# State-branch input matrices of a two-layer encoder: built transposed from table rows in scratch memory

## The chip, the cores and the metric

One core of one Trainium2 chip runs the whole kernel. The metric is the device time of one execution in microseconds (us), shown as the median of several runs. Engines are named as in the profile: PE is TensorE (PEld its weight loads), DVE is VectorE, ACT is ScalarE, POOL is GpSimd, SP is SyncE. L457 is line 457 of the kernel before.

## The reference, cut to what matters

An encoder of two layers over 512 tokens of width 2048, all float32. Each layer normalises, projects to 10272 columns, runs two token mixers side by side, a gated delta rule and a diagonal state-space branch ("state branch"), projects both, gates and adds them, and projects once more. The change is in the state branch. Per direction `d` it computes

```python
ug = u.reshape(bsz, L, N_GROUPS_B, S5_GROUP_CH)          # 64 groups of 16 channels
lam_bar = exp(lam * dt)                                   # complex, 64 states a group
b_bar = ((lam_bar - 1.0) / lam)[..., None] * (b_re + 1j * b_im)
bu = einsum('gpc,blgc->blgp', b_bar[d], ug)
states = associative_scan(_ssm_combine, (lam_bar, bu), axis=1, reverse=...)
y += einsum('gcp,blgp->blgc', c[d], states).real
```

## The kernel before, in words

**Dense products.** Every projection is cut into tiles of 128 output channels by 512 tokens. For each slice of 128 inputs there are three matmuls (L122, L123, L124), since weights and activations are split into a high and a low part in a reduced float32 format. `_weights` (L91) loads 8 slices of weights (`w_raw`, SP's queue, two buffers), ACT rounds them (`w_hi`, L65) and DVE takes the rest (`w_lo`, L66), three buffers each. A product fills one of three `acc` buffers in PSUM.

**The state branch** (`_s5`, L339) is traced at a raised priority beside the dense products, and the framework's scheduler writes one fixed order of instructions for each engine from modelled durations; an engine runs its list in order. Only the start, the delta-rule scan with its filler products, and the finish have PE's order written out by hand. Tokens are taken in 64 chunks of 8, so that only 64 steps of the recurrence are left. The 64 groups go in two halves (`hf`) of 32. In a half:

- *Parameters* (L361 to L424): `lam_in` and `b_in` are loaded; about 80 small DVE operations (`_exp_poly`, `_sincos`, L372 to L391) give the decay `lam_bar` and the scaled input matrix `b_bar`; the loop at L412 makes the powers 0 to 8 of `lam_bar`. All tiles have (real or imaginary, state) on the 128 partitions and (direction, group) along them.
- *Input matrices* (L445 to L464): eight sets `q` of four groups. For each direction `gen` (L429) multiplies `b_bar` with eight powers into `e_m`, of which the partitions are states. A matmul needs (lag, channel) on the partitions, so PE transposes each group's 128 by 128 block with the identity (L457, `ps_et`), ACT copies the four blocks back (`e_t`, L459), and `_halves` (L271) multiplies them with the input chunk `u_ch` into `ps_e`; ACT copies that to the state tile `h_st` (L464).
- *Recurrence* (L477 to L484): 64 steps of five small DVE operations.
- *Outputs* (L485 to L538): `gen` again for the output matrices `c_l`, short convolution kernels through a scratch tensor `d_k`, and products `ps_y`.

A half has its own pools of SBUF, in the memory that the half before or the last layer's final tiles leave free. All loads and stores of this branch and of the delta rule go through POOL's queue (`c.q`), in one fixed order: among them the stores `d_u` and `d_qk` of freshly projected tiles and the loads of the delta-rule scan.

**After it** come query, key and value tiles with a short convolution on DVE (`_qkv`), `_delta_pre`, `_delta_inv`, 46 gate tiles, the delta-rule scan (`_delta_scan`, L713) with other dense products between its steps, and last (L1128 on) the products with `w_pa` and `w_out`, whose split activations `m_h` and `m_l` take 64 KB of each partition.

Of the kernel before, what the change touches and what calls it, by code (L numbers as in the profile page):

```python
# [15 lines left out]
F32 = mybir.dt.float32  # L16
# [3 lines left out]
ALU = mybir.AluOpType  # L20
# [316 lines left out]

@with_exitstack
def _s5(ctx, c, l):  # L339
# [3 lines left out]
    HG = NG // 2  # L343
    pss = ctx.enter_context(tc.tile_pool(name=f"pss{l}", bufs=3, space=PSUM, reuse_waits="tile"))
    LOH, HIH = slice(0, 64), slice(64, 128)
    for hf in range(2):
        with ExitStack() as es:
            sp = es.enter_context(tc.tile_pool(name=f"s5_{l}_{hf}", bufs=1, reuse_waits="tile"))
            PW = [128, 2, HG]
            H = sp.tile([128, 2, HG, 65], F32, name="h_st")  # L350
            lr = sp.tile(PW + [9], F32, name="lam_r")
            lq = sp.tile(PW + [9], F32, name="lam_q")
            bp = sp.tile([128, 2, HG + 1, 16], F32, name="b_bar")
            bb = bp[:, :, 0:HG, :]
# [4 lines left out]
            bs = wk.tile(PW + [16], F32, name="b_swap", bufs=1)
            with tc.tile_pool(name=f"s5p_{l}_{hf}", bufs=1, reuse_waits="tile") as pp:  # L360
                lam = pp.tile([128, 3, 2, HG], F32, name="lam_in")  # L361
                b_in = pp.tile([128, 2, 2, HG, 16], F32, name="b_in")
                with tc.issue_after(c.x_load.ins) if (l, hf) == (0, 0) else nullcontext():
                    q = nc.sync if (l, hf) == (0, 0) else c.q
                    q.dma_start(out=lam, in_=i["s5_lam"][l, hf])
                    q.dma_start(out=b_in, in_=i["s5_b"][l, hf])
                mk = lambda nm: pp.tile(PW, F32, name=nm)
                re, im, ld = lam[:, 0], lam[:, 1], lam[:, 2]
                dt, t0, t1, mag = mk("p_dt"), mk("p_t0"), mk("p_t1"), mk("p_mag")
                l1r, l1i, fr, fi = mk("p_lr"), mk("p_li"), mk("p_fr"), mk("p_fi")  # L370
                _exp_poly(nc, pp, dt, ld, "d")
                V.tensor_tensor(out=t0, in0=re, in1=dt, op=ALU.mult)  # L372
                _exp_poly(nc, pp, mag, t0, "m")
                V.tensor_tensor(out=t0, in0=im, in1=dt, op=ALU.mult)
                _sincos(nc, pp, l1i, l1r, t0, "a")
                V.tensor_tensor(out=l1r, in0=l1r, in1=mag, op=ALU.mult)
                V.tensor_tensor(out=l1i, in0=l1i, in1=mag, op=ALU.mult)

                V.tensor_tensor(out=t0, in0=re, in1=re, op=ALU.mult)
                V.tensor_tensor(out=t1, in0=im, in1=im, op=ALU.mult)  # L380
                V.tensor_tensor(out=t0, in0=t0, in1=t1, op=ALU.add)
                V.reciprocal(out=dt, in_=t0)
                V.tensor_scalar(out=mag, in0=l1r, scalar1=-1.0, scalar2=None, op0=ALU.add)
                V.tensor_tensor(out=t0, in0=mag, in1=re, op=ALU.mult)
                V.tensor_tensor(out=t1, in0=l1i, in1=im, op=ALU.mult)
                V.tensor_tensor(out=t0, in0=t0, in1=t1, op=ALU.add)
                V.tensor_tensor(out=fr, in0=t0, in1=dt, op=ALU.mult)
                V.tensor_tensor(out=t0, in0=l1i, in1=re, op=ALU.mult)
                V.tensor_tensor(out=t1, in0=mag, in1=im, op=ALU.mult)
                V.tensor_tensor(out=t0, in0=t0, in1=t1, op=ALU.subtract)  # L390
                V.tensor_tensor(out=fi, in0=t0, in1=dt, op=ALU.mult)  # L391

                S16 = PW + [16]
                W16 = [128, 2, HG, 16]
                bt = bs
                sg = mk("p_sg")
                V.tensor_scalar(out=sg[LOH], in0=fi[LOH], scalar1=-1.0, scalar2=None, op0=ALU.mult)
                V.tensor_copy(out=sg[HIH], in_=fi[HIH])
                bcf = lambda a: _bc(a.unsqueeze(3), W16)
                V.tensor_tensor(out=bb, in0=b_in[:, 0], in1=bcf(fr), op=ALU.mult)  # L400
                V.tensor_tensor(out=bt, in0=b_in[:, 1], in1=bcf(sg), op=ALU.mult)
                V.tensor_tensor(out=bb, in0=bb, in1=bt, op=ALU.add)
                V.tensor_copy(out=bs[LOH], in_=bb[HIH])
                V.tensor_copy(out=bs[HIH], in_=bb[LOH])

                li = pp.tile(PW + [9], F32, name="lam_i")
                V.memset(lr[:, :, :, 0:1], 1.0)
                V.memset(li[:, :, :, 0:1], 0.0)
                V.tensor_copy(out=lr[:, :, :, 1], in_=l1r)
                V.tensor_copy(out=li[:, :, :, 1], in_=l1i)  # L410
                for k in range(2, 9):
                    a, b = k // 2, k - k // 2  # L412
                    V.tensor_tensor(out=t0, in0=lr[:, :, :, a], in1=lr[:, :, :, b], op=ALU.mult)
                    V.tensor_tensor(out=t1, in0=li[:, :, :, a], in1=li[:, :, :, b], op=ALU.mult)
                    V.tensor_tensor(out=lr[:, :, :, k], in0=t0, in1=t1, op=ALU.subtract)
                    V.tensor_tensor(out=t0, in0=lr[:, :, :, a], in1=li[:, :, :, b], op=ALU.mult)
                    V.tensor_tensor(out=t1, in0=li[:, :, :, a], in1=lr[:, :, :, b], op=ALU.mult)
                    V.tensor_tensor(out=li[:, :, :, k], in0=t0, in1=t1, op=ALU.add)
                neg = lambda o, a: V.tensor_scalar(out=o, in0=a, scalar1=-1.0, scalar2=None, op0=ALU.mult)
                neg(lq[LOH], li[LOH])  # L420
                V.tensor_copy(out=lq[HIH], in_=li[HIH])
                V.tensor_copy(out=q8[LOH], in_=li[LOH, :, :, 8])
                neg(q8[HIH], li[HIH, :, :, 8])
                V.tensor_copy(out=l8, in_=lr[:, :, :, 8])  # L424
# [4 lines left out]
            def gen(out, a, p, b, q, gs, d, ks, kn):  # L429
# [14 lines left out]
            h0 = H[:, 0, 0, 0:1]  # L444
            for q in range(8):  # L445
                j, g0 = hf * 4 + q // 2, q * 4
                gs = slice(g0, g0 + 4)
                if q % 2 == 0:
                    u = load_u(j)
                pe = pss.tile([128, 2, 4, 64], F32, name="ps_e", tag="ps")  # L450
                for d in range(2):
                    E = wk.tile([128, 4, 8, 16], F32, name="e_m", tag="e_m")
                    ks = slice(7, None, -1) if d == 0 else slice(0, 8)
# [31 lines left out]
            def kernels(jl):  # L485
# [13 lines left out]
                for q in range(2):  # L499
                    gl = slice(q * 4, q * 4 + 4)  # L500
                    gs = slice(jl * 8 + q * 4, jl * 8 + q * 4 + 4)
                    for d in range(2):
                        cm = C[q, d] = wk.tile([128, 4, 9, 16], F32, name=f"c_l{q}{d}", tag="c_l", bufs=CLB)
                        ks = slice(0, 9) if d == 0 else slice(8, None, -1)
                        gen(cm, ci[:, 0, d, gl], lr, ci[:, 1, d, gl], lq, gs, d, ks, 9)
# [446 lines left out]
def hybrid_encoder_kernel(ctx: ExitStack, tc: tile.TileContext, i: dict, out: bass.AP, dbg=None):  # L952
# [14 lines left out]
    c.d_u = dt("d_u", [8, 8, 128, 64])  # L967
    c.d_k = dt("d_k", [8, 2, 4, 32, 240])
# [70 lines left out]
    for l in range(DEPTH):  # L1039
# [142 lines left out]
def _layout(inp):  # L1182
# [43 lines left out]
    lam = np.empty((L, 2, 2, 64, 3, 2, 32), np.float32)  # L1226
    for q, nm in enumerate(("lam_re", "lam_im", "log_dt")):
        a = f[nm] if nm != "log_dt" else np.broadcast_to(f[nm][..., None], f["lam_re"].shape)
        a = a.reshape(L, 2, 2, 32, 64).transpose(0, 2, 4, 1, 3)
        lam[:, :, :, :, q] = a[:, :, None]  # L1230
# [50 lines left out]
```

## Time and profile before

| | us |
|---|---|
| median of 3 runs | 3087.45 |
| lowest, highest | 3082.66, 3088.57 |
| the profiled execution's own time | 3085.16 |
| its span, first to last instruction | 3083.3 |
| mean granted clock of TensorE, as a share of full speed | 0.995 |

The profile is one execution. "Busy" is the time in which an engine had an instruction running, except that matmuls overlap and their ends are modelled: a row's mean for one matmul is longer than what one adds to a dense stream. An engine's idle time matters only if that engine sets the end.

### The profile page before, as it was taken

The numbers are of one execution on the slowest core, as the hardware profiler recorded it, in microseconds if no ns is written. First come the engines' busy times: TensorE is split into PE (matmuls) and PEld (weight loads), VectorE is DVE, ScalarE is ACT, GpSimd is POOL, SyncE is SP. The second block draws the span as 40 slices with busy tenths as digits, with TensorE's granted clock in tenths as the row PEclk, the third lists the DMA queues.
The fourth block names the chain that finished last, engine by engine and source line by source line (L and its number), as shares of the span: only waits on it lengthen the run. The fifth ranks groups of instructions, "written<-read, shape, count | busy, mean of one in ns | idle before, by whom it ended". The sixth has DMA issues, their size and how long they took to land. (4 is left out here: it accounts for less than half of the span.)

```text
span 3083.3 us, 45415 instructions
## 1 busy us (share of the span) xinstructions
PE 3014.7 (98%) x17398; PEld 2387.5 (77%) x17398; DVE 2288.5 (74%) x4299; ACT 1016.7 (33%) x1310; POOL 435.8 (14%) x718
## 2 busy tenths in 40 slices
PE   9999999999999999999999999999999999999998
PEld 7777788777888777888887677877778877788887
DVE  8899969898698476543487998889968964765433
ACT  4343334333322332222323334343332223422222
POOL 1010112322000331000010102032230012300000
PEclk9999999999999999999999999999999999999999
DMA  6243345665433766644433324466554356666433
GB/s 205 93 140 103 129 154 176 204 185 156 148 123 124 246 200 201 239 165 141 150 112 97 130 103 147 141 180 206 171 171 142 118 188 182 213 215 217 154 120 113
DMA packets 199801, 493.49 MB, mean 160 GB/s; under 512 B 58848, under 2 KB 63424, under 8 KB 198560
## 3 DMA queue, kind: packets, MB, share of 16 engines
q1 hardware_dynamic: 154416, 345.84, 33.6%
q0 software_dynamic: 45024, 144.74, 15.3%
q8 instruction: 137, 2.24, 0.3%
q14 instruction: 80, 0.66, 0.1%
q10 hardware_dynamic: 144, 0.01, 0.0%
HBM read 381.64 MB, written 108.86 MB: 159 GB/s over the span
## 5 line engine op out<-in xcount | busy, mean ns | idle before, releaser
L122 PE MATMUL acc<-act,w_hi 128*128 128x512 f32 x3200 | 1280.8, 400 | 6.2 <-DVE cv_pre L546 3.9
L124 PE MATMUL acc<-act,w_lo 128*128 128x512 f32 x3200 | 1272.4, 398 | 2.4 <-DVE w_lo L66 2.3
L123 PE MATMUL acc<-act,w_hi 128*128 128x512 f32 x3200 | 1269.7, 397 | 0.0
L65 ACT CAST w_hi<-w_raw 128x1024 fp32r<-128x1024 f32 (+1 forms) x467 | 488.1, 1045 | 1160.9 <-PE acc L123 856.0
L66 DVE TENSOR_TENSOR w_lo<-w_raw,w_hi 128x1024 fp32r<-128x1024 f32 (+1 forms) x465 | 567.2, 1220 | 259.6 <-ACT w_hi L65 257.2
L122 PEld LDWEIGHTS acc<-act,w_hi 128*128 128x128 f32 x3200 | 603.7, 189 | 156.2 <-issue 14.1
L124 PEld LDWEIGHTS acc<-act,w_lo 128*128 128x128 f32 x3200 | 603.2, 188 | 149.1 <-issue 7.3
L123 PEld LDWEIGHTS acc<-act,w_hi 128*128 128x128 f32 x3200 | 603.8, 189 | 137.8 <-issue 4.2
L122 PE MATMUL acc<-m_l,w_hi 128*128 128x512 f32 (+1 forms) x528 | 205.2, 389 | 0.0
L124 PE MATMUL acc<-m_h,w_lo 128*128 128x512 f32 (+1 forms) x528 | 204.9, 388 | 0.0
L123 PE MATMUL acc<-m_h,w_hi 128*128 128x512 f32 (+1 forms) x528 | 204.9, 388 | 0.0
L550 DVE SCALAR_TENSOR_TENSOR cv_y<-cv_pre,cw,cv_y 128x510 f32<-128x510 f32 (+1 forms) x192 | 142.8, 747 | 7.5 <-ACT cv_y L548 5.5
L122 PEld LDWEIGHTS acc<-m_l,w_hi 128*128 128x128 f32 x528 | 99.1, 188 | 22.7
L124 PEld LDWEIGHTS acc<-m_h,w_lo 128*128 128x128 f32 x528 | 99.1, 188 | 22.7
L123 PEld LDWEIGHTS acc<-m_h,w_hi 128*128 128x128 f32 x528 | 99.2, 188 | 22.5
L703 DVE TENSOR_TENSOR x_inv<-x_inv,x_tmp 128x62 f32<-128x62 f32 (+30 forms) x124 | 106.4, 858 | 2.8
L701 DVE TENSOR_TENSOR x_tmp<-x_inv 128x62 f32<-128x62 f32 (+30 forms) x124 | 106.3, 857 | 2.8
L1164 DVE TENSOR_TENSOR x_res<-x_res,acc 128x512 f32<-128x512 f32 x31 | 21.3, 688 | 104.4 <-PE acc L124 83.5
L1078 DVE TENSOR_TENSOR z_t<-acc,rstd_b 128x512 f32<-128x512 f32 x96 | 66.1, 689 | 41.7 <-PE acc L124 41.1
L1148 DVE TENSOR_TENSOR g_in<-acc,g_in 128x512 f32<-128x512 f32 x32 | 22.2, 692 | 80.3 <-PE acc L124 80.3
L518 POOL DMA_DIRECT2D m_l<-d_k x128 | 67.4, 534 | 70.4 <-PE ps_y L271 36.8
L484 DVE TENSOR_TENSOR h_st<-h_st,st_a 128x64 f32<-128x64 f32 x256 | 70.5, 275 | 5.2
(358 smaller groups left out, 3094.5 us busy)
## 6 DMA issues: line engine op xcount, KB each, us to landing
w_raw<-in_w_in_dram SPq DMA_DIRECT2D x319, 512.0 KB, 3.7
w_raw<-in_w_out_dram SPq DMA_DIRECT2D x64, 512.0 KB, 3.7
d_keqe<-k_e POOLq DMA_DIRECT2D x32, 512.0 KB, 4.4
d_g<-z_t SPq DMA_DIRECT2D x64, 256.0 KB, 2.1
w_raw<-in_w_pb_dram SPq DMA_DIRECT2D x32, 512.0 KB, 3.6
g_in<-d_g SPq DMA_DIRECT2D x64, 256.0 KB, 3.3
w_raw<-in_w_pa_dram SPq DMA_DIRECT2D x32, 512.0 KB, 4.1
ke_s<-d_keqe POOLq DMA_DIRECT2D x56, 256.0 KB, 4.5
```

The source lines that it names most:

```text
L65: nc.scalar.copy(out=hi, in_=src)
L66: nc.vector.tensor_tensor(out=lo, in0=src, in1=hi.bitcast(F32), op=ALU.subtract)
L122: c.nc.tensor.matmul(acc, wh[:, q, :], lo(k), start=k == 0, stop=False)
L123: c.nc.tensor.matmul(acc, wh[:, q, :], hi(k), start=False, stop=False)
L124: c.nc.tensor.matmul(acc, wl[:, q, :], hi(k), start=False, stop=k == nk - 1)
L484: V.tensor_tensor(out=hs(n + 1), in0=hs(n + 1), in1=a, op=ALU.add)
L518: c.q.dma_start(out=M[s_ * 16:(s_ + 1) * 16].rearrange("p g t c -> p g (t c)"), in_=c.d_k[l][j][:, :, 0:16, (7 - s_) * 16:(15 - s_) * 16]. ...
L550: nc.vector.scalar_tensor_tensor(out=y[:, o0:o1], in0=pre[:, i0:i0 + o1 - o0], scalar=cw[:, tap:tap + 1], in1=y[:, o0:o1], op0=ALU.mult, o ...
L701: V.tensor_tensor(out=t, in0=_bc(X[:, k + 1:, k:k + 1], [128, n, k]), in1=_bc(X[:, k:k + 1, 0:k], [128, n, k]), op=ALU.mult)
L703: V.tensor_tensor(out=X[:, k + 1:, 0:k], in0=X[:, k + 1:, 0:k], in1=t, op=ALU.add)
L1078: V.tensor_tensor(out=z, in0=acc, in1=c.rstd, op=ALU.mult)
L1148: V.tensor_tensor(out=ga, in0=acc, in1=ga, op=ALU.mult)
```

## The change

The parameters of a layer are computed once for both halves, in a new function `_s5_tables`, now with (half, direction, group) on the partitions and states along them. For layer 0 it is called at the start of `_s5`, for layer 1 right after layer 0's delta-rule scan. It stores two kinds of tables to scratch memory: rows for the input matrices (`d_lam`, the powers of the decay; `d_bb`, the scaled input matrix), and, after 34 transposes on PE, the state-major form that recurrence and outputs use (`d_lt5`, `d_bt5`). In `_s5` each half loads the state-major tables, and each set `q` loads its rows by four DMAs whose sources repeat: a row of powers goes to the 16 partitions of its lag, a row of the input matrix to each of the 8 lags. Three DVE operations then give the input matrices of both directions with (lag, channel) on the partitions, and PE multiplies them without transposing. `_layout` arranges `s5_lam` and `s5_b` on the host to suit. The recurrence and the outputs are as before, except that `gen` reads its powers from the loaded table.

```diff
+def _s5_tables(c, l):
...
+        with tc.issue_after(c.x_load.ins) if l == 0 else nullcontext():
+            q = nc.sync if l == 0 else c.q
+            q.dma_start(out=lam, in_=i["s5_lam"][l])
+            q.dma_start(out=bb, in_=i["s5_b"][l])
...
+        for n in (1, 2, 4):
+            x, y, W = slice(1, n + 1), slice(n + 1, 2 * n + 1), [128, n, 64]
...
+            V.tensor_tensor(out=lr[:, y], in0=a, in1=b, op=ALU.subtract)
...
+        nc.scalar.copy(out=pw[:, :, 0], in_=lr)
+        nc.scalar.mul(out=pw[:, :, 2], in_=li, mul=-1.0)
+        for h in range(2):
+            for d in range(2):
+                r = slice(64 * h + 32 * d, 64 * h + 32 * d + 32)
+                if d == 0:
+                    for k in range(8):
+                        c.q.dma_start(out=c.d_lam[l][h, d, 7 - k], in_=pw[r, k, 1:4])
+                else:
+                    c.q.dma_start(out=c.d_lam[l][h, d].rearrange("k g r p -> g k (r p)"),
+                                  in_=pw[r, 0:8, 1:4].rearrange("g k r p -> g k (r p)"))
...
+        t = pp.tile([128, 8, 2, 64], F32, name="p_bt")
+        W = [128, 8, 2, 64]
+        for q in range(2):
+            x = bb[:, q * 8:q * 8 + 8]
+            V.tensor_tensor(out=t, in0=x[:, :, ::-1], in1=_bc(fi.unsqueeze(1), W), op=ALU.mult)
+            V.tensor_tensor(out=x, in0=x, in1=_bc(fr.unsqueeze(1).unsqueeze(1), W), op=ALU.mult)
+            V.tensor_tensor(out=x, in0=x, in1=t, op=ALU.add)
+        for h in range(2):
+            for d in range(2):
+                r = slice(64 * h + 32 * d, 64 * h + 32 * d + 32)
+                c.q.dma_start(out=c.d_bb[l][h, d].rearrange("c g r p -> g c (r p)"),
+                              in_=bb[r].rearrange("g c r p -> g c (r p)"))
+        lt = pp.tile([128, 9, 2, 128], F32, name="lam_t")
+        for k in range(0, 9, 2):
...
+                    nc.tensor.transpose(ps[:, a, z], pw[:, k + a, 2 * z:2 * z + 2].rearrange("g r p -> g (r p)"), c.ident)
+            nc.scalar.copy(out=lt[:, k:k + n], in_=ps[:, 0:n])
+        bt = pp.tile([128, 128, 16], F32, name="b_t")
+        for k in range(0, 16, 4):
...
+                nc.tensor.transpose(ps[:, a], bb[:, k + a].rearrange("g r p -> g (r p)"), c.ident)
+            nc.scalar.copy(out=bt[:, :, k:k + 4].rearrange("p g c -> p c g"), in_=ps)
+        for h in range(2):
+            r = slice(64 * h, 64 * h + 64)
+            c.q.dma_start(out=c.d_lt5[l][h].rearrange("p k g -> p k g"), in_=lt[:, :, :, r].rearrange("p k z g -> p (k z) g"))
+            c.q.dma_start(out=c.d_bt5[l][h], in_=bt[:, r].rearrange("p g c -> p (g c)"))
...
 def _s5(ctx, c, l):
...
+    if l == 0:
+        _s5_tables(c, l)
...
+            c.q.dma_start(out=lt.rearrange("p k z d g -> p (k z) (d g)"), in_=c.d_lt5[l][hf])
...
+            c.q.dma_start(out=bp[:, :, 0:HG].rearrange("p d g c -> p d (g c)"),
+                          in_=c.d_bt5[l][hf].rearrange("p (d x) -> p d x", d=2))
...
+            def rows(t, d, src, ap):
+                c.q.dma_start(out=t[:, d].rearrange("p g r x -> p (g r x)"),
+                              in_=bass.AP(tensor=src.tensor, offset=src.offset, ap=ap))
             for q in range(8):
...
+                L = wk.tile([128, 2, 4, 3, 64], F32, name="l_rows", tag="l_rows")
+                B = wk.tile([128, 2, 4, 2, 64], F32, name="b_rows", tag="b_rows")
+                for d in range(2):
+                    rows(L, d, c.d_lam[l][hf, d, 0, g0:g0 + 1], [[HG * 192, 8], [0, 16], [1, 768]])
+                    rows(B, d, c.d_bb[l][hf, d, 0, g0:g0 + 1], [[0, 8], [HG * 128, 16], [1, 512]])
+                L, B = [x.rearrange("p d g r x -> p (d g) r x") for x in (L, B)]
+                E = wk.tile(W8, F32, name="e_m", tag="e_m")
+                t = wk.tile(W8, F32, name="e_t", tag="e_t", bufs=1)
+                V.tensor_tensor(out=E, in0=B, in1=_bc(L[:, :, 0:1], W8), op=ALU.mult)
+                V.tensor_tensor(out=t, in0=B[:, :, ::-1], in1=L[:, :, 1:3], op=ALU.mult)
+                V.tensor_tensor(out=E, in0=E, in1=t, op=ALU.add)
                 pe = pss.tile([128, 2, 4, 64], F32, name="ps_e", tag="ps")
                 for d in range(2):
-                    E = wk.tile([128, 4, 8, 16], F32, name="e_m", tag="e_m")
...
-                    gen(E, bb[:, d, gs], lr, bs[:, d, gs], lq, gs, d, ks, 8)
-                    pt = pss.tile([128, 4, 128], F32, name="ps_et", tag="ps")
                     for g in range(4):
-                        nc.tensor.transpose(pt[:, g, :], E[:, g].rearrange("p s c -> p (s c)"), c.ident)
-                    et = wk.tile([128, 4, 128], F32, name="e_t", tag="e_t")
-                    nc.scalar.copy(out=et, in_=pt)
-                    for g in range(4):
-                        _halves(c, pe[:, d, g, :], et[:, g, :], u[:, (q % 2) * 4 + g, :], True, True)
+                        _halves(c, pe[:, d, g, :], E[:, d * 4 + g].rearrange("p r x -> p (r x)"),
+                                u[:, (q % 2) * 4 + g, :], True, True)
...
             fill = _Fill(filler())
             _delta_scan(c, l, fill)
             fill.run()
+        if l + 1 < DEPTH:
+            _s5_tables(c, l + 1)
```

## Rows read from the trace of the kernel before

**Rows 1.** The page: its span, and busy time of each engine.

```profile
span 3083.3 us, 45415 instructions
...
PE 3014.7 (98%) x17398; PEld 2387.5 (77%) x17398; DVE 2288.5 (74%) x4299; ACT 1016.7 (33%) x1310; POOL 435.8 (14%) x718
```

**Rows 2.** Stretches: length, busy of PE, PEld, DVE, ACT, POOL; PEclk, DMA share, GB/s.

```profile
80.00:120.00 40.00, 40.00 (x250) 29.99 (x249) 32.32 (x61) 10.15 (x16) 3.22 (x4) 1.00 0.34 100
...
280.00:400.00 120.00, 113.71 (x808) 88.06 (x808) 109.95 (x271) 44.68 (x59) 18.09 (x32) 1.00 0.38 123
500.00:560.00 60.00, 60.00 (x541) 47.93 (x540) 49.90 (x81) 29.14 (x44) 18.45 (x27) 1.00 0.59 178
640.00:760.00 120.00, 114.10 (x701) 89.27 (x701) 107.78 (x294) 38.59 (x47) 34.32 (x54) 1.00 0.57 171
1040.00:1160.00 120.00, 110.67 (x864) 85.83 (x865) 84.57 (x115) 46.06 (x69) 39.59 (x71) 0.97 0.68 206
1720.00:1760.00 40.00, 32.34 (x167) 24.48 (x165) 37.98 (x98) 15.86 (x23) 2.96 (x6) 0.87 0.34 117
...
2160.00:2280.00 120.00, 115.00 (x711) 88.61 (x710) 107.22 (x290) 40.26 (x49) 34.07 (x53) 1.00 0.57 173
```

**Rows 3.** Groups of PE by line: busy us, mean ns | idle before.

```profile
L271 PE MATMUL ps_e<-u_ch,e_t 128*64 128x64 f32 x1024 | 40.7, 226 | 0.0
...
L457 PE MATMUL ps_et<-k_ident,e_m 128*128 128x128 f32 x256 | 38.3, 279 | 0.0
```

**Rows 4.** Timeline of PE around four transposes: start us, us, instruction.

```profile
128.69 0.39 PE L122 MATMUL acc<-act,w_hi 128*128 128x512 f32 x1
128.92 0.39 PE L123 MATMUL acc<-act,w_hi 128*128 128x512 f32 x1
129.15 0.60 PE L457 MATMUL ps_et<-k_ident,e_m 128*128 128x128 f32 x4
129.50 0.48 PE L124 MATMUL acc<-act,w_lo 128*128 128x512 f32 x1
129.82 0.40 PE L122 MATMUL acc<-act,w_hi 128*128 128x512 f32 x1
```

**Rows 5.** Groups of DVE and ACT by line: busy us, mean ns | idle before.

```profile
L433 DVE TENSOR_TENSOR e_m<-b_bar,lam_r 128x512 f32<-128x512 f32 x64 | 42.9, 689 | 27.1 <-PE ps_et L457 26.7
...
L413 DVE TENSOR_TENSOR p_t<-lam_r 128x64 f32<-128x64 f32 x28 | 7.9, 281 | 0.8
...
L400 DVE TENSOR_TENSOR b_bar<-b_in,p_fr 128x1024 f32<-128x1024 f32 x4 | 4.9, 1216 | 0.0
...
L379 DVE TENSOR_TENSOR p_t<-lam_in 128x64 f32<-128x64 f32 x4 | 0.9, 218 | 0.0
...
L459 ACT COPY e_t<-ps_et 128x512 f32<-128x512 f32 x64 | 36.3, 586 | 74.1 <-PE ps_et L457 74.0
```

**Rows 6.** DMA issues (KB each, median us to landing), and POOL's time to issue one.

```profile
w_raw<-in_w_in_dram SPq DMA_DIRECT2D x319, 512.0 KB, 3.7
...
ke_s<-d_keqe POOLq DMA_DIRECT2D x56, 256.0 KB, 4.5
u_ch<-d_u POOLq DMA_DIRECT2D x32, 256.0 KB, 3.4
...
b_in<-in_s_b_dram POOLq DMA_DIRECT2D x3, 1024.0 KB, 5.9
...
L518 POOL DMA_DIRECT2D m_l<-d_k x128 | 67.4, 534 | 70.4 <-PE ps_y L271 36.8 <-issue 16.7 <-DMA d_k<-k_f 9.2
```

**Rows 7.** The transposes in two of the four stages: PE, PEld, ACT busy; clock, DMA.

```profile
90.00:170.00 80.00, 9.62 (x64) 7.30 (x64) 8.47 (x15) 1.00 0.29 93
500.00:560.00 60.00, 9.12 (x60) 6.73 (x60) 8.64 (x15) 1.00 0.59 178
```

**Rows 8.** Who waited for whom: us in all, times, longest us.

```profile
PE ps_T L808 <- ACT o_tok L850: 8.3, 2, 4.3
...
PE acc L122 <- DVE cv_pre L546: 3.9, 1, 3.9
```

More of the change, by code (lines that the diff above doesn't have):

```diff
@@ L335, in _sincos @@
     V.tensor_tensor(out=c_out, in0=c_out, in1=t, op=ALU.subtract)
+def _s5_tables(c, l):
+    nc, tc, i = c.nc, c.tc, c.i
+    V = nc.vector
+    with tc.tile_pool(name=f"s5t_{l}", bufs=1, reuse_waits="tile") as pp, \
+            tc.tile_pool(name=f"pst_{l}", bufs=3, space=PSUM, reuse_waits="tile") as pst:
+        PW = [128, 64]
+        lam = pp.tile([128, 3, 64], F32, name="lam_in")
+        bb = pp.tile([128, 16, 2, 64], F32, name="b_in")
+        with tc.issue_after(c.x_load.ins) if l == 0 else nullcontext():
+            q = nc.sync if l == 0 else c.q
+            q.dma_start(out=lam, in_=i["s5_lam"][l])
+            q.dma_start(out=bb, in_=i["s5_b"][l])
+        mk = lambda nm: pp.tile(PW, F32, name=nm)
+        re, im, ld = lam[:, 0], lam[:, 1], lam[:, 2]
+        dt, t0, t1, mag = mk("p_dt"), mk("p_t0"), mk("p_t1"), mk("p_mag")
+        pw = pp.tile([128, 9, 4, 64], F32, name="lam_pw")
+        lr, li = pw[:, :, 1], pw[:, :, 3]
+        l1r, l1i = lr[:, 1], li[:, 1]
+        fr = mk("p_fr")
+        fi = pp.tile([128, 2, 64], F32, name="p_fi")
+        _exp_poly(nc, pp, dt, ld, "d")
+        V.tensor_tensor(out=t0, in0=re, in1=dt, op=ALU.mult)
+        _exp_poly(nc, pp, mag, t0, "m")
+        V.tensor_tensor(out=t0, in0=im, in1=dt, op=ALU.mult)
+        _sincos(nc, pp, l1i, l1r, t0, "a")
+        V.tensor_tensor(out=l1r, in0=l1r, in1=mag, op=ALU.mult)
+        V.tensor_tensor(out=l1i, in0=l1i, in1=mag, op=ALU.mult)
+        V.memset(lr[:, 0], 1.0)
+        V.memset(li[:, 0], 0.0)
+        p0 = pp.tile([128, 4, 64], F32, name="p_w0")
+        p1 = pp.tile([128, 4, 64], F32, name="p_w1")
+        for n in (1, 2, 4):
+            x, y, W = slice(1, n + 1), slice(n + 1, 2 * n + 1), [128, n, 64]
+            br, bi = _bc(lr[:, n:n + 1], W), _bc(li[:, n:n + 1], W)
+            a, b = p0[:, 0:n], p1[:, 0:n]
+            V.tensor_tensor(out=a, in0=lr[:, x], in1=br, op=ALU.mult)
+            V.tensor_tensor(out=b, in0=li[:, x], in1=bi, op=ALU.mult)
+            V.tensor_tensor(out=lr[:, y], in0=a, in1=b, op=ALU.subtract)
+            V.tensor_tensor(out=a, in0=lr[:, x], in1=bi, op=ALU.mult)
+            V.tensor_tensor(out=b, in0=li[:, x], in1=br, op=ALU.mult)
+            V.tensor_tensor(out=li[:, y], in0=a, in1=b, op=ALU.add)
+        nc.scalar.copy(out=pw[:, :, 0], in_=lr)
[9 more added lines that the diff above has]
+                                  in_=pw[r, 0:8, 1:4].rearrange("g k r p -> g k (r p)"))
+        V.tensor_tensor(out=t0, in0=re, in1=re, op=ALU.mult)
+        V.tensor_tensor(out=t1, in0=im, in1=im, op=ALU.mult)
+        V.tensor_tensor(out=t0, in0=t0, in1=t1, op=ALU.add)
+        V.reciprocal(out=dt, in_=t0)
+        V.tensor_scalar(out=mag, in0=l1r, scalar1=-1.0, scalar2=None, op0=ALU.add)
+        V.tensor_tensor(out=t0, in0=mag, in1=re, op=ALU.mult)
+        V.tensor_tensor(out=t1, in0=l1i, in1=im, op=ALU.mult)
+        V.tensor_tensor(out=t0, in0=t0, in1=t1, op=ALU.add)
+        V.tensor_tensor(out=fr, in0=t0, in1=dt, op=ALU.mult)
+        V.tensor_tensor(out=t0, in0=l1i, in1=re, op=ALU.mult)
+        V.tensor_tensor(out=t1, in0=mag, in1=im, op=ALU.mult)
+        V.tensor_tensor(out=t0, in0=t0, in1=t1, op=ALU.subtract)
+        V.tensor_tensor(out=fi[:, 1], in0=t0, in1=dt, op=ALU.mult)
+        V.tensor_scalar(out=fi[:, 0], in0=fi[:, 1], scalar1=-1.0, scalar2=None, op0=ALU.mult)
+        t = pp.tile([128, 8, 2, 64], F32, name="p_bt")
[12 more added lines that the diff above has]
+        for k in range(0, 9, 2):
+            n = min(2, 9 - k)
+            ps = pst.tile([128, 2, 2, 128], F32, name="ps_lt", tag="ps")
+            for a in range(n):
+                for z in range(2):
+                    nc.tensor.transpose(ps[:, a, z], pw[:, k + a, 2 * z:2 * z + 2].rearrange("g r p -> g (r p)"), c.ident)
+            nc.scalar.copy(out=lt[:, k:k + n], in_=ps[:, 0:n])
+        bt = pp.tile([128, 128, 16], F32, name="b_t")
+        for k in range(0, 16, 4):
+            ps = pst.tile([128, 4, 128], F32, name="ps_bt", tag="ps")
+            for a in range(4):
+                nc.tensor.transpose(ps[:, a], bb[:, k + a].rearrange("g r p -> g (r p)"), c.ident)
[4 more added lines that the diff above has]
+            c.q.dma_start(out=c.d_bt5[l][h], in_=bt[:, r].rearrange("p g c -> p (g c)"))
@@ L357, in _s5 @@
             es2 = ExitStack()
             wk = es2.enter_context(tc.tile_pool(name=f"s5e_{l}_{hf}", bufs=2, reuse_waits="tile"))
[L359 to L424, printed above, removed]
@@ L1224, in _layout @@
     o["d_skip"] = dsk.reshape(L, 128, 16)
[L1226 to L1230, printed above, removed]
-    o["s5_lam"] = lam.reshape(L, 2, 128, 3, 2, 32)
-    b = np.empty((L, 2, 2, 64, 2, 2, 32, 16), np.float32)
-    for ri in range(2):
-        for q in range(2):
-            a = f[("b_re", "b_im")[(ri + q) % 2]].reshape(L, 2, 2, 32, 64, 16).transpose(0, 2, 4, 1, 3, 5)
-            b[:, :, ri, :, q] = a
-    o["s5_b"] = b.reshape(L, 2, 128, 2, 2, 32, 16)
+    rows = lambda a: a.reshape(L, 2, 2, 32, *a.shape[3:]).swapaxes(1, 2).reshape(L, 128, *a.shape[3:])
+    ldt = np.broadcast_to(f["log_dt"][..., None], f["lam_re"].shape)
+    o["s5_lam"] = A(np.stack([rows(a) for a in (f["lam_re"], f["lam_im"], ldt)], axis=2))
+    o["s5_b"] = A(np.stack([rows(f[nm]).swapaxes(2, 3) for nm in ("b_re", "b_im")], axis=3))
     cc = np.empty((L, 8, 2, 64, 2, 2, 8, 16), np.float32)
```

27 lines of the change are left out of this document (15 added, 12 removed).

## Prediction

> **What bounds the kernel now.** First the page's busy table: PE is busy for 3014.7 of 3083.3 us, DVE for 2288.5, ACT and POOL far less [rows 1]. So PE is the bound, with 68.6 us idle. A busy PE need not be a productive one, so I read next, in equal stretches, where the idle time lies [rows 2]. In the stretches where input matrices are built (80 to 120 us and 500 to 560 us) PE is busy all of the time: nothing there makes it wait, and each thing taken out of its list shortens the list. It idles elsewhere: beside the recurrence, where DVE is busy nine tenths of the time (6.3 us in 280 to 400, 5.9 in 640 to 760, 7.7 in 1720 to 1760, 5.0 in 2160 to 2280), and in the delta-rule scan (9.3 us in 1040 to 1160). [...] Last the list of PE's waits: the longest sum is 8.3 us, two waits on a copy of the scan [rows 8]; no transpose, no matrix of the input and no DMA stands high in it.
>
> **Transposes, the term that counts.** The change takes 256 transposes off PE (2 layers x 2 halves x 8 sets x 2 directions x 4 groups). Their group has 38.3 us busy, 279 ns each [rows 3]. This is not their price, because matmuls overlap. The price is read from the spacing of starts [rows 4]: from one L123 at 128.92 to the second dense matmul after the transposes at 129.82 pass 0.90 us; two dense matmuls alone take 2 x 0.23 (128.69 to 128.92). The four transposes and the switch to them and back cost 0.90 - 0.46 = 0.44 us. The tables add 34 transposes a layer (18 of powers, 16 of the input matrix), 68 in all, of the same size. From 64 groups of four, 47 are left as saving: 47 x 0.44 = **20.7 us**. The products `ps_e` (1024, 40.7 us busy [rows 3]) stay as they are, only with another tile as weights.
>
> [...]
>
> **DVE and ACT, not in the sum.** A half's parameters are now some 80 operations of 0.22 us, 42 for the powers of 0.28, three of 1.22 and a few copies [rows 5], about 17.6 + 11.8 + 3.7 + 3 = 36 us, four times over. New: the same 80, then 18 for the powers (up to four times as wide, some 0.4 us) and six of 1.22, 17.6 + 7 + 7.3 = 32 us, twice. The matrices themselves cost 64 x 3 x 0.689 = 132 us and will cost 32 x 3 x 1.22 = 117 us, 1.22 being the row of 1024 elements. DVE loses 80 + 15 = 95 us of 2288. ACT loses 64 copies (36.3 us) and gets 22 of like size (13 us). Neither sets the end where PE is full, so I book nothing; what less DVE work may do to PE's idle time is a rival below.
>
> **POOL and DMA.** POOL issues 52 table stores, 8 table loads, 128 row loads and 2 parameter loads, and drops 6: 184 more, at 0.534 us [rows 6] about 98 us, against 436 busy of 3083 [rows 1]. Costed at nothing, since POOL idles six sevenths of the time. But its queue is in order: a row load waits until DVE has released the buffer of two sets before, and behind it stand stores of `d_u` and `d_qk`, whose tiles PE's `acc` buffers depend on. Nothing of the kind made PE wait before but one wait of 3.9 us [rows 8].
>
> Rows loaded with a repeating source are not in the trace. A set is 2 x (384 + 256) KB = 1.28 MB. Lower bound: the four overlap and land like `u_ch`, 3.4 us; upper bound: one after another at 4.5 each, 18 us [rows 6]. I take 7.5 us, by scaling `b_in` (1024 KB on the same queue, 5.9 us), the nearest in size. The stages took 80 us and 60 us for eight sets [rows 7], 7.5 to 10 us a set, and two sets of buffers let the loads run ahead. So the loads are hidden at 7.5 and not at 18. All rows are 42 MB, a twelfth of what is moved, beside a DMA share of 0.34 and 0.59 in those stretches [rows 2].
>
> **Where the tables are made.** Layer 0: DVE's part is some 4 us shorter, but rows go out to scratch and come back, some 3.4 + 7.5 us; the first matrix is 0 to 7 us later. PE goes on with input tiles and the first query and key tiles, as it does now: nothing. Were that cover gone, 7 us. Layer 1: between the scan of layer 0 and its last products, nine rounds of four transposes and one ACT copy (0.44 + 0.59) and a store of 3.4 us, 13 us, stand before `m_h` gets its memory. Three `acc` buffers of 24 dense matmuls hold 3 x 24 x 0.23 = 16.6 us: nothing; 13 if it isn't covered. DVE work of the tables may also fall into the scan. Below nothing, too: layer 1 no longer computes parameters while its input tiles run, so that its recurrence can start sooner.
>
> **Sum.** 3085.2 of the profiled execution less 20.7 is 3064.5. The median of the runs is 2.3 us above that execution, so **3067 us**.
>
> **Rivals.** *Stalls shrink as well.* DVE is near full where PE idles [rows 2]; 95 us less may take half of those four stretches' 24.9 us of idle and the 5.2 us of clock, 15 us more: 3052. For it: the waits there are on DVE. Against: the recurrence itself, which fills DVE there, is unchanged, and the order on each engine is written anew.
>
> *A transpose costs what its row says,* 188 x 0.279 = 52 us: 3035. Against it is the spacing in rows 4. [...]
>
> *Given back.* The saving is spent in new waits at the layer boundary (13 us) and the first matrix (7): about 3087.
>
> *Slower: input matrices come late on PE.* PE's place for the 32 sets of products is fixed by modelled times; what they wait for depended on DVE and PE alone, and would depend on a landing of 1.28 MB. If rows land late, PE stands at the products with dense work behind them that can't pass. At 20.7 / 32 = 0.65 us per set the gain is gone; at 1.5 us per set the kernel takes 3067 + 48 = 3115. For it: the second half's stage already has a DMA share of 0.59 [rows 2]. Against: `u_ch` comes by the same queue for the same products, and PE shows no wait on it; ahead-loading covers two sets. [...]
>
> **How the numbers follow.** A measurement of this kernel can tell about 0.2%, 6 us, from no change. Forecast, the PE saving within some 10 us of stall changes: 0.57. Stalls shrink: 0.15. Row price: 0.02. Given back, 3081 to 3093: 0.13. Late matrices: 0.13. The first three are faster: 0.74; same 0.13; slower 0.13. The range leaves out the row price, the far end of the second case and most of the last, so it goes from 3045 (all 30 us of the four stretches gone would be 3037) to 3088.
>
> **What would show it.** Right: `ps_et` gone and 68 transposes with `ps_lt` and `ps_bt`; PE's busy time down by about the sum; PE full where input matrices are built; no wait of `ps_e` on DVE's `e_m` over a microsecond in all. Wrong: waits of `ps_e` on `e_m`, with `e_m` waiting on the DMA of rows; idle PE at the start of the `w_pa` products; longer waits on `cv_pre` or on `w_hi` for its load; a second stretch at half clock. Were PE's work down by 20 us and the time not, the idle time of rows 2 would have grown by as much.

## The result, and the profile after

The changed kernel takes 3164.4 us (median of 4 runs, 3158.26 to 3168.43) against 3085.05 us (3081.06 to 3088.57): ratio 1.0256, 95% interval 1.0230 to 1.0281. It is 79 us slower; 20 us faster was forecast.

The page of the changed kernel: span, busy times, and the line of POOL's DMA queue (packets, MB, share of 16 engines).

```profile
span 3158.7 us, 44770 instructions
...
PE 3014.3 (95%) x17210; PEld 2383.0 (75%) x17210; DVE 2212.2 (70%) x3865; ACT 999.3 (32%) x1276; POOL 546.6 (17%) x902
...
q0 software_dynamic: 67360, 197.05, 22.9%
```

Against [rows 1] the span is 75.4 us longer, PE has 188 instructions fewer and the same busy time, and its idle time went from 68.6 to 144.4 us. DVE lost 76 us of work (95 was told ahead), and it bought nothing. Where the idle time lies, the equal stretches show (length, PE busy and instructions, PEclk, DMA share, GB/s):

```profile
120.00:160.00 40.00, 36.53 (x210) 1.00 0.94 195
160.00:200.00 40.00, 35.99 (x281) 0.96 0.98 232
200.00:240.00 40.00, 36.91 (x247) 1.00 0.42 141
480.00:520.00 40.00, 35.29 (x231) 0.91 1.01 276
520.00:560.00 40.00, 29.87 (x234) 0.87 0.97 245
1320.00:1360.00 40.00, 27.74 (x121) 0.87 0.80 231
1600.00:1640.00 40.00, 29.80 (x218) 0.83 0.88 204
1640.00:1680.00 40.00, 30.68 (x212) 0.79 0.75 185
1960.00:2000.00 40.00, 26.93 (x213) 0.91 0.94 205
2000.00:2040.00 40.00, 33.92 (x239) 0.87 0.70 174
```

All but the line at 1320 are stretches in which input matrices are built, where PE was full before ([rows 2], 80 to 120 and 500 to 560). The ten lines hold 10.6 + 14.8 + 12.3 + 19.5 + 19.2 = 76.4 us of idle time: as much as is new. In the same stretches the DMA share goes up to 1.01, where [rows 2] had 0.34 and 0.59, and the granted clock is down to 0.79 at worst: a part of them ran at half clock after PE had stood idle. PE stands from 1607.7 to 1613.8 us, for one; the granted clock is 1.00 up to 1610, 0.50 from 1612 to 1616 and 1.00 again from 1618, and the starts of the dense matmuls lie 0.43 us apart at 0.50 (1614.39 to 1614.81), 0.23 before. The mean granted clock fell from 0.995 to 0.985. The account is: idle +75.8; transposes gone, by the prediction's price, -20.7; and a remainder of +20.3. Work done at the lower clock fits that remainder: by the two means it can cost at most 0.015 x 3158.7 - 0.005 x 3083.3 = 32 us.

The lists of waits, of PE and of DVE (us in all, times, longest):

```profile
PE ps_e L271 <- DVE e_m L512: 29.5, 13, 5.1
PE acc L122 <- DVE g_in L1210: 12.3, 1, 12.3
...
PE ps_e L271 <- DMA u_ch<-d_u: 5.2, 2, 3.2
```

```profile
DVE e_m L510 <- DMA b_rows<-d_bb: 83.8, 22, 10.5
DVE e_t L511 <- DMA b_rows<-d_bb: 16.2, 3, 6.1
```

One such wait on DVE and on PE, from their timelines (start, us, instruction, idle time before it). A row tile lands late, DVE needs the rows for its first operation, and PE meets the set with its dense work behind it:

```profile
530.25 1.23 DVE L510 TENSOR_TENSOR e_m<-b_rows,l_rows 128x1024 f32<-128x1024 f32 x1 [5.92 <-DMA b_rows<-d_bb]
...
533.66 1.22 DVE L512 TENSOR_TENSOR e_m<-e_m,e_t 128x1024 f32<-128x1024 f32 x1
```

```profile
530.34 0.40 PE L122 MATMUL acc<-act,w_hi 128*128 128x512 f32 x1
534.94 1.38 PE L271 MATMUL ps_e<-u_ch,e_m 128*64 128x64 f32 x32 [4.20 <-DVE e_m L512]
```

The four stages hold 64.1 us of idle time (76.4 without the 12.3 at 1320). At `ps_e` itself PE stands for 38.1 of them: 29.6 for `e_m`, 5.2 for `u_ch`, 3.3 without a named wait. The other 26.0 us it stands at other products. DVE's list is in order, so while DVE waits for rows it makes nothing else either: the three longest of those other waits, 15.2 us, come right behind such a wait. The longest is for the low part of a weight (PE, then DVE):

```profile
1613.80 0.79 PE L124 MATMUL acc<-act,w_lo 128*128 128x512 f32 x1 [6.12 <-DVE w_lo L66]
```

```profile
1610.40 1.23 DVE L511 TENSOR_TENSOR e_t<-b_rows,l_rows 128x1024 f32<-128x1024 f32 x1 [6.09 <-DMA b_rows<-d_bb]
...
1612.52 1.22 DVE L66 TENSOR_TENSOR w_lo<-w_raw,w_hi 128x1024 fp32r<-128x1024 f32 x1
```

The landing times (KB each, median us), where [rows 6] had 3.4 for `u_ch` and 5.9 for 1024 KB of `b_in`:

```profile
w_raw<-in_w_in_dram SPq DMA_DIRECT2D x319, 512.0 KB, 4.0
...
l_rows<-d_lam POOLq DMA_DIRECT2D x64, 384.0 KB, 13.0
b_rows<-d_bb POOLq DMA_DIRECT2D x64, 256.0 KB, 12.9
```

### The profile page after: what moved, and what is told of

The parts are those of the page before. It is cut to its first block, busy times and chain, and to the rows that moved or that the text cites. A ratio compares the mean times of both kernels' runs of the same rounds, so it can differ in the third digit from the quotient of the medians.

```text
span 3158.7 us, 44770 instructions
## 1 busy us (share of the span) xinstructions
PE 3014.3 (95%) x17210; PEld 2383.0 (75%) x17210; DVE 2212.2 (70%) x3865; ACT 999.3 (32%) x1276; POOL 546.6 (17%) x902
## 3 DMA queue, kind: packets, MB, share of 16 engines
q0 software_dynamic: 67360, 197.05, 22.9%
## 5 line engine op out<-in xcount | busy, mean ns | idle before, releaser
L122 PE MATMUL acc<-act,w_hi 128*128 128x512 f32 x3200 | 1286.5, 402 | 15.3 <-DVE g_in L1210 12.3
L510 DVE TENSOR_TENSOR e_m<-b_rows,l_rows 128x1024 f32<-128x1024 f32 x32 | 39.2, 1225 | 89.5 <-DMA b_rows<-d_bb 83.8
L271 PE MATMUL ps_e<-u_ch,e_m 128*64 128x64 f32 x1024 | 43.2, 248 | 38.1 <-DVE e_m L512 29.5
L271 PEld LDWEIGHTS ps_e<-u_ch,e_m 128*64 128x64 f32 x1024 | 38.9, 159 | 50.7 <-issue 30.5
```

Source lines behind the costliest of these rows:

```text
L122: c.nc.tensor.matmul(acc, wh[:, q, :], lo(k), start=k == 0, stop=False)
L271: c.nc.tensor.matmul(out[r], w[:, r], x, start=start, stop=stop)
L510: V.tensor_tensor(out=E, in0=B, in1=_bc(L[:, :, 0:1], W8), op=ALU.mult)
```

## Experiments

**Undoing a part.** In *rows once* the rows are loaded for the first set of a half only and used for all eight, so the powers and inputs of seven sets are those of other groups.

```diff
-                L = wk.tile([128, 2, 4, 3, 64], F32, name="l_rows", tag="l_rows")
...
+                if q == 0:
+                    L = wk.tile([128, 2, 4, 3, 64], F32, name="l_rows", tag="l_rows")
...
```

> Each half loads its table rows for the first set only and builds all eight sets from them (the other seven sets' own rows are left out); DVE, ACT and PE keep every instruction. Theory, row loads land late and PE stands at the input products: 28 of 32 loads go, so the waits on e_m and the half-clock stretches they cause go with them, about 85 us: 3080, that is 3085 - 20.7 for the transposes + 17 for the wait before the w_pa products, which stays. Rival, the new instruction order or the table step is what costs: over 3130.

Measured: 3087.97 us, ratio 1.0019 [1.0010, 1.0029]. The wait of `ps_e` on `e_m` is down to one of 0.9 us, and 76 us are back. If the saving of 20.7 us is there, the losses to explain are 79 + 21 = 100 us, and the row loads are three quarters of them. The boundary wait on `g_in` stays, 10.7 us.

*Tables late* computes layer 1's tables at the start of its own `_s5`; all is computed.

```diff
-    if l == 0:
-        _s5_tables(c, l)
+    _s5_tables(c, l)
...
-        if l + 1 < DEPTH:
-            _s5_tables(c, l + 1)
```

> Layer 1 makes its tables at its own start, as layer 0 does, and nothing stands between the scan and the w_pa products of layer 0. Theory, the 12.3 us wait there comes from the tables' memory and chain: that wait and its half-clock stretch go, 17 us, 3147. Rival, it was covered or moves: layer 1's first matrix comes some 50 us later in exchange, PE waits there instead, 3160 to 3185.

Measured: 3130.47 us, ratio 1.0151 [1.0136, 1.0166]. The wait on `g_in` is gone; the row loads still land in 13.2 us. The gain is 34 us and not 17: DVE's first wait on rows also fell, from 83.8 to 60.8 us. That came with a new order of layer 1, and why was not settled.

*Transposes kept* has the tables, computed once, but builds the matrices as before: `gen`, 256 transposes, ACT's copies, no rows.

```diff
-                    rows(L, d, c.d_lam[l][hf, d, 0, g0:g0 + 1], [[HG * 192, 8], [0, 16], [1, 768]])
...
+                    gen(E, bp[:, d, gs], bs[:, d, gs], gs, d, ks, 8)
...
                     for g in range(4):
...
+                        nc.tensor.transpose(pt[:, g, :], E[:, g].rearrange("p s c -> p (s c)"), c.ident)
...
+                    nc.scalar.copy(out=et, in_=pt)
...
```

> The tables once a layer stay, but the input matrices are built from the state-major tables and transposed on PE as before: no row loads by the sets. Theory, late rows cost the time: 3085 + 7.5 for the 68 transposes of the tables + 17 for the wait before the w_pa products = 3110, PE without waits where input matrices are built. Rival, parameters once a layer gain by themselves through DVE: under 3095. Rival, the table step costs beyond its 17 us: over 3125.

Measured: 3112.36 us, ratio 1.0095 [1.0080, 1.0110], as expected; PE waits 15.2 us on `g_in`. So computing tables once, where the change puts them, loses some 29 us by itself (its pair of medians: 3112.36 and 3082.95). The boundary is half of it, and the 68 added transposes 7.5 us by the prediction's price.

**What makes the rows slow.** *Distinct rows*: only the sources differ, 128 stretches at one distance; every engine's list is the same.

```diff
-    rows(L, d, c.d_lam[l][hf, d, 0, g0:g0 + 1], [[HG * 192, 8], [0, 16], [1, 768]])
-    rows(B, d, c.d_bb[l][hf, d, 0, g0:g0 + 1], [[0, 8], [HG * 128, 16], [1, 512]])
+    rows(L, d, c.d_lam[l][hf, 0, 0, 0:1], [[768, 128], [1, 768]])
+    rows(B, d, c.d_bb[l][hf, 0, 0, 0:1], [[1024, 128], [1, 512]])
```

> The same row loads, as many bytes and as many issues in the same order, but the 128 partitions of a load read 128 different stretches of the same table instead of one row 16 or 8 times (so the matrices are built from other rows). Theory A, the repeated reading of one address range makes the loads slow: landing falls from 13 to 8 us or less and the time to 3120 or less. Theory B, the bytes alone fill the DMA engines: landing stays at 12 us or more, the time within 10 us of 3164.

Measured: 3073.46 us, ratio 0.9969 [0.9956, 0.9981]: 91 us less than the change, from the addresses alone. Its page: the queue's line, two landings; and the stretch 480 to 560, which was 65.16 us busy at 0.89 of the clock with a DMA share of 0.99:

```profile
q0 software_dynamic: 59168, 196.99, 20.4%
...
l_rows<-d_lam POOLq DMA_DIRECT2D x64, 384.0 KB, 6.1
b_rows<-d_bb POOLq DMA_DIRECT2D x64, 256.0 KB, 6.7
```

```profile
480.00:560.00 80.00, 80.00 (x572) 1.00 0.78 272
```

The same bytes take the DMA engines 0.204 x 3070.6 = 626 us in place of 0.229 x 3158.7 = 723. So the price of these loads hangs on the form of their source. But the run changed more than one thing: rows are no longer read again and again, the source is nested otherwise, and the stretches of `l_rows` now lie in one piece.

*Only the decay's rows distinct* (the first of the two lines above):

> Only the loads of the powers read 128 different stretches (the matrices are built from other powers); the input-matrix rows are still read 8 times each. If each repeated load brings its own slowness, the powers' landing falls to about 7 us and the input rows keep more than 9, time between 3073 and 3164, near 3110. If only the powers' 16 readers of a row matter, all as in the run with distinct rows: 3075 to 3085. If only the input rows matter (16 of them 16384 bytes apart), time stays over 3140.

Measured: 3111.39 us, ratio 1.0087 [1.0072, 1.0102]; landings 9.0 and 9.7. A little over half the way. The source of `b_rows` is the change's own and yet lands 3.2 us sooner, so the two loads delay each other.

*Padded pitch* gives the tables one more group a row (`NG // 2 + 1`), in case the powers of two in their distance hurt.

> Every instruction as in the changed kernel, in the same order; only the tables in scratch memory have one group more per row, so that rows lie 25344 and 16896 bytes apart instead of 24576 and 16384. Theory A, the loads are slow because rows at that distance from each other meet in the same part of the memory: landing falls from 13 us towards the 6 to 7 of the distinct rows, time towards 3073 to 3110. Theory B, it is the same row being read by several engines at once: landing stays at 12 or more, time within 10 us of 3164.

Measured: 3161.45 us, ratio 1.0252 [1.0236, 1.0267], landings 13.0 and 12.8. A power of two in the distance is not the cause.

*Four copies* stores each table four times, so that a row has a quarter of the readers. Here and below, the sources of `l_rows` and `b_rows` stand side by side, taken from their two lines.

```diff
-    [[HG * 192, 8], [0, 16], [1, 768]]      [[0, 8], [HG * 128, 16], [1, 512]]
+    [[HG * 192, 32], [0, 4], [1, 768]]      [[0, 2], [HG * 128, 64], [1, 512]]
```

> Four copies of both tables are stored, and a load's partitions share them out: 4 readers of a row instead of 16, 2 instead of 8; the matrices are those of the changed kernel. Costs 22 more stores a layer and 5.4 MB, which delay layer 0's first matrix. If the number of readers of a row is the cause: landing 6 to 9 us, time 3075 to 3100 (the wait of 17 us before the w_pa products stays). If reading one small stretch of memory at a time is slow however often a row is read: landing over 11, time over 3150.

Measured: 3190.5 us, ratio 1.0347 [1.0331, 1.0362]; landings 13.0 and 13.7, and PE waits 35.1 us on `g_in`; the stores of the row tables carry four times the bytes. The number of readers fell and nothing landed sooner. The fastest `l_rows` took 2.9 us, the fastest `b_rows`, whose source now has 2 on its outermost level, 8.8.

That pointed to the outermost count. *Distinct, written 8 by 16* has nearly the stretches of the distinct run (neighbours share 16 elements at most) but nests them (steps of 752 and 1008 elements in place of 768 and 1024):

```diff
+    [[12288, 8], [752, 16], [1, 768]]       [[16384, 8], [1008, 16], [1, 512]]
```

> The complement of the run with the channel outermost: 128 different stretches are read, as in the run with distinct rows, but written as 8 by 16, so that the outermost source count is 8 (the matrices are built from other rows). Theory, the count of 8 is what slows the loads: landing 12 us or more, time 3150 to 3170. Rival, repeated reading: landing 6 to 8 us and 3070 to 3085.

Measured: 3164.56 us, ratio 1.0262 [1.0249, 1.0276], the change's own time, without repeated reading. Its page:

```profile
q0 software_dynamic: 67360, 197.05, 22.6%
...
l_rows<-d_lam POOLq DMA_DIRECT2D x64, 384.0 KB, 13.1
b_rows<-d_bb POOLq DMA_DIRECT2D x64, 256.0 KB, 13.0
```

So the nesting makes the loads slow, and not the repetition. The queue's packets are 67360 here and in the change, 59168 in the distinct run: 8192 more, 64 for each of the 128 row loads. In the changed kernel's trace these are 8192 packets of 8 bytes. *Only the decay's rows distinct*, where `b_rows` alone has 8 on the outermost level, has half of them (63264 packets in all); the run written 16 by 8, below, has none (59168); *four copies*, with 32 and 2, has 91040, the packets of its added stores among them. So the outermost count changes how a load is divided. The small packets are not the loss, some 12 ns each in the changed kernel's trace: by the queue's share of 16 engines, the other 59168 packets took 192 ns in the mean here, 169 in the distinct run. Why a load that is divided so lands later is not shown.

*Distinct, written 16 by 8* asks for the rest of the way:

```diff
+    [[6144, 16], [752, 8], [1, 768]]        [[8192, 16], [1008, 8], [1, 512]]
```

> The input matrices' rows come from stretches that do not overlap, as in the distinct runs, but the source is written as 16 outer by 8 inner (the powers and inputs are so of other table rows). If the channel-outer run's remaining distance of 32 us from the first distinct run is the 16 by 8 shape of the source, this run is slow in the same way: row landing about 9 us, about 3105 us, ratio 1.007. If it is repeated reading of the same table rows, landing is about 6.5 us and the time about 3073, ratio 0.997.

Measured: 3098.95 us, ratio 1.0051 [1.0036, 1.0066]:

```profile
l_rows<-d_lam POOLq DMA_DIRECT2D x64, 384.0 KB, 8.2
b_rows<-d_bb POOLq DMA_DIRECT2D x64, 256.0 KB, 8.9
```

This and the run before have the same inner steps over the same memory, and differ in how the 128 are divided: the median of `l_rows` goes from 13.1 to 8.2. To the distinct run's 128 it goes on to 6.1. What makes that second part stays open, for the distinct run also has other steps, and its `l_rows` come from one piece of memory.

**Repairs.** *Channel outer* swaps the order on the partitions to (channel, lag), in the two row sources and `u_ch` alike, so that the outermost count is 16. It computes all that the change computes.

```diff
+    [[0, 16], [HG * 192, 8], [1, 768]]      [[HG * 128, 16], [0, 8], [1, 512]]
```

> The input matrices and the input chunk they meet have (channel, lag) on the partitions instead of (lag, channel): a load's source is 16 channels by 8 lags, so its outermost count is 16 and no longer 8. Every row is still read 16 or 8 times, and every engine's list is the same. [...] Rival, repeated reading of the same rows is slow: landing 12 or more, time within 10 us of 3164.

Measured: 3105.38 us, ratio 1.0070 [1.0056, 1.0083]; landings 8.7 and 9.3; `ps_e` still waits 9.4 us on `e_m`, and 14.7 us go on `g_in`. 59 of the 79 us are back; the author's estimate was 3070 to 3085. The distance of 6 us from the 16 by 8 run above is about what repeated reading costs at most; the intervals of the two ratios overlap.

*Tables aside* moves layer 1's tables ahead, behind `_delta_inv`, with memory of their own.

```diff
...
         _delta_inv(c, l)
+        if l + 1 < DEPTH:
+            _s5_tables(c, l + 1)
...
```

> Layer 1's tables are made in the memory beside the delta rule's own, called right behind the inversion and ahead of the gate tiles, where DVE and POOL have room; the row loads are those of the changed kernel. Theory, the wait of 12.3 us before the w_pa products and its half clock come from the place of the tables: both go, 17 us, 3147, and no wait on g_in over 1 us. Rival, the tables now delay the inversion or the delta-rule scan: 3155 to 3180.

Measured: 3194.17 us, ratio 1.0357 [1.0340, 1.0375]. The wait on `g_in` is gone and a dearer one takes its place:

```profile
PE ps_V L883 <- DMA t_i<-d_ti: 26.4, 1, 26.4
PE ps_lt L429 <- ACT lam_pw L383: 10.3, 1, 10.3
```

*Channel outer and tables late* puts the two repairs together.

> As the run with the channel outermost, and layer 1 makes its tables at its own start. If the two costs add: 3073 - 17 for the wait before the w_pa products, 3050 to 3060, faster than both kernels. Rival, layer 1's first matrix comes too late and PE waits there instead: 3070 to 3090.

Measured: 3081.61 us, ratio 0.9995 [0.9986, 1.0004], 11 runs: as fast as the kernel before, no faster, where 3050 to 3060 was expected if the two costs add. Its list of PE's waits begins with 8.1 us of the old cause:

```profile
PE ps_e L271 <- DVE e_m L511: 8.1, 3, 4.2
```

Three more versions go on from it; none gains. *Rows of two* leaves out the third part of the decay's rows (a fourth DVE operation takes the sign) and adds a third buffer:

> The channel-outer version with late tables, with the decay table's rows cut from three parts to two (real, minus imaginary: a third fewer bytes of that load, four vector operations in place of three for the set) and a third buffer for both row tiles. The whole computation is kept. If what is left of the wait is the bytes and the two buffers, the row loads land in about 7 us, the matrices' wait on TensorE goes from 8 us to near nothing, and the time is about 3070 us, ratio 0.995. If the landing is set by something else (the order on the queue, or VectorE's added operations), it stays at 3080, ratio 1.00.

Measured: 3095.98 us, ratio 1.0037 [1.0025, 1.0049]. The decay's rows land in 8.9 us, no sooner than before in spite of a third fewer bytes; what they gained is seen only beside the next run, which has the third buffer alone.

*Third buffer* alone (`bufs=3` for both row tiles):

> The channel-outer version with late tables, with a third buffer for both row tiles and nothing else changed. The whole computation is kept. If the remaining 8 us of waits for the matrices are there because loads start only when the tile of two sets before is free, they go, and the time is about 3072, ratio 0.996. If the third buffer only lets one more landing overlap the others, or the new order moves stalls elsewhere (as the run with rows of two), it stays within 5 us of 3081, ratio 1.00.

Measured: 3124.72 us, ratio 1.0138 [1.0122, 1.0154], worse. With three buffers in place of two more loads are in flight and each lands later, 11.1 and 11.6 us; with fewer bytes (the run before) it is 8.9 and 9.4. That fits loads bound by their rate, and not by when they may start. And the framework wrote a new order: the first row load goes out at 163.5 us in place of 112.5, and PE stands in the delta-rule scan, 21.9 us.

```profile
PE ps_V L882 <- DMA t_i<-d_ti: 21.9, 4, 9.9
PE ps_e L271 <- DVE e_m L511: 16.1, 10, 5.4
```

*Rows on ACT's queue* (`nc.scalar` in place of `c.q` in `rows`):

> The channel-outer version with late tables, the 128 row loads issued from ACT's queue in place of POOL's. The whole computation is kept. If the landing of 8.6 to 9.5 us holds a part that belongs to POOL's queue (its stores ahead of a load, its way of issuing), it falls to about 7 us and the time to about 3072, ratio 0.996. If it is the transfer itself, landing stays at 9 us, and ACT, which now stands in its list until VectorE gives a row tile free, is late with the rounding of weights: 3085 to 3100, ratio 1.00 to 1.005.

Measured: 3096.49 us, ratio 1.0051 [1.0034, 1.0068]; landings 8.1 and 9.4, about as before (8.6 and 9.5), so nothing that belongs to POOL's queue alone holds them; PE now waits 10.4 us on ACT (`ps_qk` on `qk_sq`).

**Both costs away.** *Distinct and late* joins the distinct sources to the late tables:

> Rows from 128 stretches of equal distance as in the first distinct run (powers and inputs are those of other table rows), and layer 1's tables at the start of its own state branch. All engines' lists but POOL's addresses are those of the run with late tables. If slow rows and the boundary tables are the whole of what went wrong, both are gone here and the saving of the transposes alone is left: 3085 less the predicted 20.7 is about 3064, ratio 0.993; by the two runs that undo one each, 3073 less 12 to 17, it is 3056 to 3061. If something else of the change costs time, this run stays at 3073 or above.

Measured: 3057.84 us, ratio 0.9915 [0.9901, 0.9930]. Its page, and the stretches in which the changed kernel stood:

```profile
span 3050.8 us, 44771 instructions
...
PE 2985.9 (98%) x17210; PEld 2363.1 (77%) x17210; DVE 2207.6 (72%) x3865; ACT 1002.8 (33%) x1278; POOL 538.6 (18%) x902
```

```profile
480.00:560.00 80.00, 80.00 (x573) 1.00 0.79 273
1960.00:2040.00 80.00, 80.00 (x597) 1.00 0.76 251
```

With rows that land in 5.9 and 6.6 us and no tables at the boundary, the forecast gain is there (23.5 us between the medians), so these two costs are the loss. This run is no version to use, since its rows are the wrong ones.

## Why the prediction was wrong, step by step

**The step that failed is the landing of the rows,** "I take 7.5 us, by scaling `b_in`". Its bounds, 3.4 and 18, held the 13.0 that came, but the value in them was chosen by size alone. `b_in`'s source and that of `u_ch` run over 128 rows; the new sources run over 8, and that, by the first distinct run and the one written 8 by 16, is worth a factor of two. The text said it itself: "hidden at 7.5 and not at 18". At 5.9 to 6.7 us they are hidden indeed (`ps_e` waits once on `e_m` in the distinct run, 0.5 us, and not at all in *distinct and late*), at 8.1 to 9.7 nearly (6.9 to 10.4 us of such waits), at 13 not.

**The rival "input matrices come late on PE"** is what happened, and it was priced too low: 1.5 us a set, 48 in all, by choice. The idle time of those stretches is 64.1 / 32 = 2.0 us a set. Its own mechanism, PE at the products `ps_e`, is 38.1 us of that, 1.2 a set. Of the rest at least 15.2 us came by a way that the price left out, DVE's list standing still for the rows. And with both came the lower clock (0.83 and 0.79 in 1600 to 1680), of which the price knew nothing. Its chance of 0.13 leaned on `u_ch` not being late, a load of another form. The weights, on SP's queue, landed little later beside the row loads: `w_raw` in 4.0 us, 3.7 before [rows 6].

**The layer boundary,** "nothing; 13 if it isn't covered": not covered, 12.3 us. The place was right (the memory of `m_h` and `m_l`), the cover was not, and the store that was put at 3.4 us took some 9.7. POOL's, DVE's and PE's timelines of the changed kernel at the boundary:

```profile
1326.14 1.10 POOL L440 DMA_DIRECT2D d_bt<-b_t  x2 [3.62 <-ACT b_t L436]
```

```profile
1336.44 1.90 DVE L66 TENSOR_TENSOR m_l<-m_in,m_h 128x512 fp32r<-128x512 f32 x3 [1.35 <-DMA d_bt<-b_t]
1341.09 1.33 DVE L1211 TENSOR_TENSOR m_in<-m_in,g_in 128x512 f32<-128x512 f32 x2 [2.76 <-DMA m_in<-d_m]
1342.47 1.33 DVE L66 TENSOR_TENSOR m_l<-m_in,m_h 128x512 fp32r<-128x512 f32 x2
1344.41 1.36 DVE L1210 TENSOR_TENSOR g_in<-acc,g_in 128x512 f32<-128x512 f32 x2 [0.61 <-DMA g_in<-d_g]
```

```profile
1345.25 0.77 PE L122 MATMUL acc<-act,w_hi 128*128 128x512 f32 x1 [12.26 <-DVE g_in L1210]
```

The two stores of the last table (`d_bt`) go out between 1326.14 and 1327.24, and DVE's first `m_l` stands until they have ended, at 1336.44; behind it in its list is `g_in`, which empties `acc`, and that in turn needs loads of `m_in` and `g_in` whose tiles the same operations free. So three full `acc` buffers were not 16.6 us of cover: the chain that drains them had to start up again after the store, 8 us from 1336.44 to 1344.41. That 12.3 comes close to the 13 is chance: the 13 was the length of the table step, and most of the 12.3 is this restart.

**The transposes, 20.7 us,** were sized right, as far as *distinct and late* shows: the medians differ by 23.5 us; PE's busy time is 28.8 us less, of which up to 9 are clock (0.998 against 0.995, over 3083 us), which leaves at least 19.6. So spacing is the price, and not the row's mean: that rival gave 3035, and the run is 23 us above it. In the changed kernel the gain is there, and hidden under the losses.

**The first matrix,** "0 to 7 us later", is much later: PE's first `ps_e` starts at 140.6 us, 100.7 before. It costs nothing: in *distinct and late* it starts at 140.9. The reason given, other work for PE, held (PE is busy all of 80 to 240 us there); the size was wrong.

**"Stalls shrink"** did not: DVE does 76 to 81 us less (95 forecast), and even in the best run PE's idle time is 64.9 us beside 68.6. The 5.2 us of clock in that rival are an estimate, 40 us times what 0.87 lacks of 1.00 [rows 2]: in the kernel before PE idles in parts from 1735 us on, and the granted clock is 0.50 from 1742 to 1750. In *distinct and late* PE's mean granted clock was 0.998, 0.995 before.

## What to carry to other kernels

When a change turns an on-chip step into a load, price the load by the shape of its source, first of all the count on its outermost level (here 384 KB landed in 13.1 us with 8, in 8.2 with 16, in 6.1 with the form of 128), and only then by its size. Ask also what else the engine that waits for the load has in its list: all of that waits too (here at least 15.2 us of PE's waits). Where a new step holds memory ahead of the next stage, count how long the chain that drains the buffers takes to start again (here 8 us), not only what the buffers hold. Here a price read from the spacing of instructions held (20.7 us, 23.5 between the medians); a price scaled from a transfer of another form is a guess, and its upper bound belongs in the forecast.

## What the runs showed that was not expected

Two sources of the same bytes differ by a factor of two in landing: outermost 8, 13.1 us; 16, 8.2; 128, 6.1 (384 KB). The slow loads also keep the DMA engines busier (share 0.99 in 480 to 560, 0.78 for the fast form, at 261 and 272 GB/s), and a third buffer makes each load land later (8.6 to 11.1). Reading one row 8 or 16 times over costs little beside it: 6 us of the whole time at most between two runs of the 16 by 8 form.
